# Latent mixer of a fused two-block kernel: value products for two query tiles at once, and a pad on the right-hand side of SBUF

## The chip, the cores and the metric

The kernel runs on one core of a Trainium2 chip. The metric is the device time of one execution in microseconds (us). Beside it stands one profiled execution, from which all rows below come. The engines are named as in the profile: PE is TensorE, PEld its weight loads, DVE VectorE, ACT ScalarE, POOL GpSimd, SP SyncE.

## The reference, cut to what matters

The program computes two blocks one after the other: first two layers of attention, mLSTM and MLP on 512 tokens, then a second block whose first mixer is multi-head latent attention and whose second is a gated linear scan. The change lies in the latent mixer. It has 16 heads, 512 tokens (`hx`) and 256 context tokens (`hc`). Queries and keys have 64 + 32 elements, values 64. The context attends to itself alone, the tokens attend to context and tokens together (768 keys):

```python
def attention_blocks(q, k, v):
...
    def one_block(qi):
        s = jnp.einsum('bqhrd,bkhd->bhrqk', qi, k, preferred_element_type=F32) * scale
        p = jax.nn.softmax(s, axis=-1).astype(v.dtype)
        return jnp.einsum('bhrqk,bkhe->bqhre', p, v)
...
def mla_mixer(hc, hx, row, col, w_in, q_norm_g, w_uq, kv_norm_g, w_ukv, w_out):
...
    oc = attention_blocks(qc, kc, vc)
    ox = attention_blocks(qx, jnp.concatenate([kc, kx], axis=1), jnp.concatenate([vc, vx], axis=1))

    def out(o, gate):
        b, n, _ = gate.shape
...
```

The result is multiplied by the gate's silu and taken through the output weight.

## The kernel before, in words

All work runs on one core, and the products carry nearly all of it. Most are made of three by `mm3` (lines 280, 281 and 282: high part by high part, high by low, low by high), each operand split into a high and a low part by `split` (lines 251 to 255). The profile shows these three lines with the names of the destination and of the operands: `S<-kT,qT` are scores, `T<-cqT,spl` the queries, `T<-ckT,spl` the keys, `A<-spl,hi` the mixer's output products.

`mla` is the latent mixer. Its attention goes through 8 pairs of heads `hp`. Each pair has five steps: a context step (`c=1`, both context query tiles at once, 256 keys) and four query tiles of 128 tokens with 768 keys (`t0` 0 to 3; called tiles 0 to 3 here, and the two heads of a pair a and b).

- `softmax` makes the scores of one head into a PSUM buffer `S` (two of them), the negated row maximum on DVE (line 1211), the exponential with its row sum on ACT (line 1216, which the profile shows as ACTIVATE and ACTIVATION_READ_ACCUMULATOR), the reciprocal and the multiply on DVE (lines 1218 and 1221), once for head a and once for head b.
- `weigh` runs one step behind. It transposes the normalised weights 128 by 128 on PE (line 1236, six for a head and a tile), copies them on ACT to `pt` (line 1237, 512 and 256 columns), and then multiplies them with the values into a quarter of the PSUM buffer `O` (line 1244: six blocks of keys by two heads, 128 columns each, head a into partitions 0 to 63 and head b into 64 to 127).
- `prepare(hp+1)` makes the queries and keys of the next pair in small pieces that are taken up between these steps. A pair with an even number has its pieces in the context step and tile 0, a pair with an odd number in tile 1 too, and pair 7 has none.

The order of each engine's instructions is set when the program is built, by the tile framework's list scheduler from the code's order and the buffers' reuse; it isn't written out by hand. Buffers on the left and right side of SBUF are stacked one beside the other: `res` is the first pool on the right (`side="right"`), so everything that is allocated there behind it stands at an offset that `res` fixes. Among these are the mixer's `cqT`, `ckT` (in place of which `hi` comes later), `V`, `sg` and the raw weights. They stand at 224 bytes past a multiple of 256.

Of the kernel before, what the change touches and what calls it, by code (L numbers as in the profile page):

```python
# [10 lines left out]
F32 = mybir.dt.float32  # L11
# [3 lines left out]
AF = mybir.ActivationFunctionType  # L15
# [181 lines left out]
class Prog:  # L197
    def __init__(self, tc, A, ctx):
        self.tc, self.nc, self.A, self.ctx = tc, tc.nc, A, ctx
        self.const = self.pool("const", 1)  # L200
        self.res = self.pool("res", 1, side="right")
        self.raw = self.pool("raw", 2, side="right")
        self.spl = self.pool("spl", 4)
        self.sm = self.pool("sm", 4)
        self.mhalf = self.const.tile([128, 4], F32, name="mhalf")
        self.nc.gpsimd.memset(self.mhalf, -0.5)
        self.zero = self.const.tile([128, 1], F32, name="zero")
        self.nc.gpsimd.memset(self.zero, 0.0)
# [841 lines left out]
def mla(P, xs, mod, H, before, keep):  # L1050

    nc, A = P.nc, P.A
# [13 lines left out]
    with ExitStack() as s1:  # L1066
# [33 lines left out]
        for j in range(8):  # L1100
            w = W().rearrange("p s (k n) -> p s k n", k=8)
            for c, o, n in PARTS:
                ps = P.bankA()[:, 0:n]
                for k in range(8):
                    P.mm3(ps, w[:, 0, k], w[:, 1, k], *H.all(k, c), k == 0, k == 7)
                v = sg[j][:, o:o + n]
# [3 lines left out]
    before.close()  # L1110
    with st as s2:
        P.psum(s2, S=(2, 2), T=(3, 1), O=(1, 1))
        kp, pp, one, qp = (P.pool(*x, s2) for x in (("m2k", 3), ("m2p", 3), ("m2o", 1), ("m2q", 4)))
        kTs = [one.tile([96, 2, 768], F32R, name=f"kT{i}") for i in (2, 3, 0, 1)]
        kTs = kTs[2:] + kTs[:2]
        tab = one.tile([128, 512], F32, name="tab")
# [1 line left out]
        V = [vp.tile([128, 1024], F32, name="V") for _ in range(6)]  # L1118
# [7 lines left out]
        for c, o, n in PARTS:  # L1126
            pt = P.bankT()
# [97 lines left out]
        def weigh(hp, c, t0, ps):  # L1225
            two, m, c0 = (2, 256, 512) if c else (1, 768, 0)
            if t0 == 0:
                weigh.o = P.bankO()
            pts = []
            for p in ps:  # L1230
                pt = kp.tile([128, 768], F32, name="pt")
                for o in range(0, two * m, 512):
                    w = min(512, two * m - o)
                    pst = P.bankT()
                    for k in range(0, w, 128):
                        nc.tensor.transpose(pst[:, k:k + 128], p[:, o + k:o + k + 128], P.ident)  # L1236
                    nc.scalar.activation(pt[:, o:o + w], pst[:, 0:w], AF.Copy)  # L1237
                pts.append(pt)
                yield
            for t in range(two):  # L1240
                for k in range(m // 128):
                    for i in range(2):
                        h = 2 * hp + i
                        nc.tensor.matmul(weigh.o[64 * i:64 * i + 64, (t0 + t) * 128:(t0 + t + 1) * 128],  # L1244
                                         V[4 * c + k][:, h * 64:(h + 1) * 64],
                                         pts[i][:, t * m + k * 128:t * m + (k + 1) * 128],
                                         start=(k == 0), stop=(k == m // 128 - 1))
            n = 256 if c else 512
            if (t0 + two) * 128 == n:
                v = sg[hp][:, c0:c0 + n]  # L1250
                nc.vector.tensor_tensor(v, v, weigh.o[:, 0:n], op=OP.mult)
# [3 lines left out]
        for hp, c, t in steps:  # L1255
            if c:
                ready = prepare(hp + 1) if hp < 7 else iter(())
            sm = softmax(hp, c, t)
            w = weigh(*before) if before else iter(())
            next(w, None)  # L1260
            for _ in range(2):
                ps = next(sm)
                next(ready, None)
                next(w, None)
            before = (hp, c, t, ps)
        alternate(weigh(*before))


# [325 lines left out]
def program(tc, A, out):  # L1594
    with ExitStack() as ctx:
        P = Prog(tc, A, ctx)
        xs = [P.res.tile([128, 1024], F32, name=f"x{t}") for t in range(4)]
        before, keep = ExitStack(), ExitStack()
        H, mod = first_block(P, xs, P.pool("hx", 1, before))
        finish = mla(P, xs, mod.m[0], H, before, keep)  # L1600
        gla(P, xs, finish, keep, mod.m[1], out)
# [18 lines left out]
```

## Time and profile before

| | |
|---|---|
| time, median of 3 runs | 2332.73 us (2332.15 to 2332.93) |
| the profiled execution | 2335.07 us |
| its span | 2333.3 us, 1.8 us less than the execution |
| PE busy in the span | 2284.1 us (98%) |
| weight loads (PEld) | 1875.9 us (80%) |
| DVE | 1478.0 us (63%) |
| ACT | 1063.0 us (46%) |
| attention of the latent mixer | from about 1686 to 1934 us |

An engine is busy while it runs an instruction; a PE row's time is that of its instruction from start to end, and neighbours overlap, so that the distance from one start to the next is what a product costs the stream. "x24" joins 24 records of one kind in a row. Each float32 product of a value group leaves two records. The granted clock of TensorE is the share of full speed.

### The profile page before, as it was taken

To read this page: it belongs to the slowest core of one execution; us is meant where nothing else is said; L and a number is where in the kernel's file an instruction comes from. 1 tells how busy PE (TensorE), PEld (TensorE's weight loads), DVE (VectorE), ACT (ScalarE), POOL (GpSimd) and SP (SyncE) were. 2 spreads that over 40 slices of the span, in tenths; PEclk is the share of its full clock that TensorE was granted. 3 is DMA by queue.
4 is the path that set the end of the run, shared out by engine and by line. 5 is a ranking of instruction groups with operands and counts; after the bars stand their busy time and mean duration, and the time that the engine had idled before them with its cause. 6 is when DMAs were issued, how large, how long until landed. Compare 5 with 4: busy or idle time off the path is not lost.

```text
span 2333.3 us, 30784 instructions
## 1 busy us (share of the span) xinstructions
PE 2284.1 (98%) x12108; PEld 1875.9 (80%) x12108; DVE 1478.0 (63%) x2556; ACT 1063.0 (46%) x1958; POOL 71.4 (3%) x120
## 2 busy tenths in 40 slices
PE   8999999999999999999999999999999999999998
PEld 6777878888888777788888888888888888788886
DVE  4477796555555547779645556564478776756586
ACT  3366423444443235642344445452477772563332
POOL 0000000000000000000000000010000000000000
PEclk9999999999999999999999999999999999999999
DMA  4221464555642322146454554212110121121112
GB/s 162 81 73 55 145 212 142 167 130 151 174 100 91 92 81 75 52 155 216 135 172 120 160 164 116 92 54 72 49 31 21 24 74 37 54 81 37 55 46 72
DMA packets 61312, 234.38 MB, mean 100 GB/s; under 512 B 8544, under 2 KB 9840, under 8 KB 54768
## 3 DMA queue, kind: packets, MB, share of 16 engines
q1 hardware_dynamic: 50512, 179.99, 23.3%
q0 software_dynamic: 3456, 25.17, 6.0%
q10 hardware_dynamic: 7200, 27.27, 3.7%
q8 instruction: 95, 1.56, 0.3%
q14 instruction: 49, 0.40, 0.1%
HBM read 227.15 MB, written 2.10 MB: 98 GB/s over the span
## 4 chain that ended last, share of the span: by engine, by line
PE 81%; DVE 10%; ACT 3%; DMA 3%; issue 2%; POOL 1%; SPq 0%; POOLq 0%; ACTq 0%; DVEq 0%
PE A L282 18%; PE A L281 18%; PE A L280 18%; PE S L280 4%; PE S L282 4%; PE S L281 4%; PE O L1244 2%; DVE spl L252 2%; PE T L1236 2%; PE O L522 1%; DMA ada<-in_ada 1%; PE S L496 1%; DVE junk L933 1%; PE T L516 1%; ACT spl L251 1%
## 5 line engine op out<-in xcount | busy, mean ns | idle before, releaser
L280 PE MATMUL A<-big,spl 128*128 128x512 f32 (+1 forms) x1280 | 482.2, 377 | 1.9 <-DVE x L768 1.2
L282 PE MATMUL A<-big,spl 128*128 128x512 f32 (+1 forms) x1280 | 481.0, 376 | 0.2 <-DVE spl L252 0.2
L281 PE MATMUL A<-big,spl 128*128 128x512 f32 (+1 forms) x1280 | 480.1, 375 | 0.0
L252 DVE TENSOR_TENSOR spl<-raw,spl 128x1024 fp32r<-128x1024 f32 (+2 forms) x265 | 317.2, 1200 | 184.0 <-ACT spl L251 182.2
L251 ACT ACTIVATE spl<-raw 128x1024 fp32r<-128x1024 f32 (+2 forms) x265 | 275.2, 1040 | 292.2 <-PE A L282 190.6
L282 PEld LDWEIGHTS A<-big,spl 128*128 128x128 f32 x1280 | 241.2, 188 | 44.6 <-issue 2.6
L280 PEld LDWEIGHTS A<-big,spl 128*128 128x128 f32 x1280 | 241.3, 189 | 43.9 <-DVE x L768 1.6
L281 PEld LDWEIGHTS A<-big,spl 128*128 128x128 f32 x1280 | 241.3, 189 | 42.5 <-issue 1.4
L252 DVE TENSOR_TENSOR spl<-quarter,spl 128x1024 fp32r<-128x1024 f32 x84 | 102.2, 1223 | 144.9 <-ACT spl L251 144.9
L280 PE MATMUL A<-spl,big 128*128 128x512 f32 (+2 forms) x480 | 182.7, 384 | 3.7 <-DVE tg L668 2.1
L281 PE MATMUL A<-spl,big 128*128 128x512 f32 (+2 forms) x480 | 182.3, 381 | 1.4 <-DVE spl L252 0.8
L282 PE MATMUL A<-spl,big 128*128 128x512 f32 (+2 forms) x480 | 181.7, 380 | 0.2 <-DVE ms L289 0.2
L251 ACT ACTIVATE spl<-quarter 128x1024 fp32r<-128x1024 f32 x84 | 88.2, 1057 | 97.4 <-PE S L282 41.1
L280 PEld LDWEIGHTS A<-spl,big 128*128 128x128 f32 x480 | 90.2, 189 | 23.2 <-DVE tg L668 3.0
L281 PEld LDWEIGHTS A<-spl,big 128*128 128x128 f32 x480 | 90.7, 189 | 18.9 <-DVE spl L252 3.4
L282 PEld LDWEIGHTS A<-spl,big 128*128 128x128 f32 x480 | 90.6, 189 | 16.7 <-issue 1.1
L280 PE MATMUL S<-spl,part 128*128 128x512 f32 x264 | 102.8, 389 | 0.0
L281 PE MATMUL S<-spl,part 128*128 128x512 f32 x264 | 102.8, 389 | 0.0
L282 PE MATMUL S<-spl,part 128*128 128x512 f32 x264 | 102.8, 389 | 0.0
L1211 DVE TENSOR_REDUCE mx<-S 128x1 f32<-128x768 f32 (+1 forms) x80 | 71.8, 900 | 26.5 <-PE S L282 25.7
L291 POOL TENSOR_TENSOR rstd<-ms,mhalf 128x1 f32<-128x1 f32 (+2 forms) x68 | 44.2, 650 | 1247.5 <-DVE ms L289 1203.2
L1237 ACT ACTIVATE pt<-T 128x512 f32<-128x512 f32 (+1 forms) x144 | 66.4, 501 | 32.4 <-PE T L1236 31.2
(442 smaller groups left out, 4349.2 us busy)
## 6 DMA issues: line engine op xcount, KB each, us to landing
raw<-in_wl SPq DMA_DIRECT2D x196, 512.0 KB, 3.7
ada<-in_ada ACTq DMA_DIRECT2D x48, 512.0 KB, 4.0
quarter<-in_wq SPq DMA_DIRECT2D x24, 1024.0 KB, 6.2
quarter<-in_wq POOLq DMA_DIRECT2D x24, 1024.0 KB, 8.7
raw<-in_gla SPq DMA_DIRECT2D x33, 512.0 KB, 3.4
raw<-in_mla SPq DMA_DIRECT2D x20, 512.0 KB, 3.5
raw<-in_mla SPq DMA_DIRECT2D x8, 384.0 KB, 3.0
qT<-rot SPq DMA_DIRECT2D x32, 96.0 KB, 2.8
```

The source lines that it names most:

```text
L251: nc.scalar.activation(hi, src, AF.Copy)
L252: nc.vector.tensor_tensor(lo, src, f32(hi), op=OP.subtract)
L280: mm(ps, lh, rh, start=start, stop=False, **more)
L281: mm(ps, lh, rl, start=False, stop=False, **more)
L282: mm(ps, ll, rh, start=False, stop=stop, **more)
L291: nc.gpsimd.tensor_tensor(r, ms, self.mhalf[:, 0:w], op=OP.pow)
L496: nc.tensor.matmul(banks[hh][:, 0:w], qT[hs, i, q], kT[hs, j, 0:w], start=(i + j == 0), stop=(i == 1))
L516: nc.tensor.transpose(psp[:, k * 128:(k + 1) * 128], p[:, k * 128:(k + 1) * 128], P.ident)
L1211: nc.vector.tensor_reduce(mx[:, 0:two], pss[:, 0:two * m].rearrange("p (t n) -> p t n", t=two), AX.X, OP.max, negate=True)
L1236: nc.tensor.transpose(pst[:, k:k + 128], p[:, o + k:o + k + 128], P.ident)
L1237: nc.scalar.activation(pt[:, o:o + w], pst[:, 0:w], AF.Copy)
L1244: nc.tensor.matmul(weigh.o[64 * i:64 * i + 64, (t0 + t) * 128:(t0 + t + 1) * 128], V[4 * c + k][:, h * 64:(h + 1) * 64], pts[i][:, t * m + ...
```

## The change

Two things are changed. First, `weigh` collects two query tiles: `pt` becomes a tile of 6 blocks of keys by 2 query tiles by 128 columns, the copies write every second block of it, and the products with the values are issued after every second query tile, with 256 moving columns (both tiles at once). In the context step the two context tiles go together in the same way. The pool of `pt` has four buffers in place of three. Second, a tile of 56 float32 columns (224 bytes) is allocated first in `res`.

```diff
@@ Prog.__init__
         self.res = self.pool("res", 1, side="right")
+
+        self.res.tile([128, 56], F32, name="pad")
         self.raw = self.pool("raw", 2, side="right")
@@ mla
-        kp, pp, one, qp = (P.pool(*x, s2) for x in (("m2k", 3), ("m2p", 3), ("m2o", 1), ("m2q", 4)))
+        kp, pp, one, qp = (P.pool(*x, s2) for x in (("m2k", 4), ("m2p", 3), ("m2o", 1), ("m2q", 4)))
@@ weigh
-            pts = []
-            for p in ps:
-                pt = kp.tile([128, 768], F32, name="pt")
+
+            if t0 % 2 == 0:
+                weigh.pts = [kp.tile([128, 6, 2, 128], F32, name="pt") for _ in range(2)]
+            pts = weigh.pts
+            for p, pt in zip(ps, pts):
                 for o in range(0, two * m, 512):
                     w = min(512, two * m - o)
                     pst = P.bankT()
                     for k in range(0, w, 128):
                         nc.tensor.transpose(pst[:, k:k + 128], p[:, o + k:o + k + 128], P.ident)
-                    nc.scalar.activation(pt[:, o:o + w], pst[:, 0:w], AF.Copy)
-                pts.append(pt)
+                    if c:
+                        d, v = pt[:, 0:2], pst.rearrange("p (t k n) -> p k t n", t=2, k=2)
+                    else:
+                        d, v = pt[:, o // 128:(o + w) // 128, t0 % 2], pst[:, 0:w].rearrange("p (k n) -> p k n", n=128)
+                    nc.scalar.activation(d, v, AF.Copy)
                 yield
-            for t in range(two):
+            if c or t0 % 2:
+                q = slice(0, 256) if c else slice((t0 - 1) * 128, (t0 + 1) * 128)
                 for k in range(m // 128):
                     for i in range(2):
                         h = 2 * hp + i
-                        nc.tensor.matmul(weigh.o[64 * i:64 * i + 64, (t0 + t) * 128:(t0 + t + 1) * 128],
-                                         V[4 * c + k][:, h * 64:(h + 1) * 64],
-                                         pts[i][:, t * m + k * 128:t * m + (k + 1) * 128],
+                        nc.tensor.matmul(weigh.o[64 * i:64 * i + 64, q], V[4 * c + k][:, h * 64:(h + 1) * 64],
+                                         pts[i][:, k].rearrange("p t n -> p (t n)"),
                                          start=(k == 0), stop=(k == m // 128 - 1))
```

The scheduler puts the work in another order around it. In the listings below an instruction has its line, destination and sources; the change adds two lines ahead of `mm3` and more within `weigh`, so that line 1244 becomes 1252, 1236 becomes 1240, and 280 to 282 become 282 to 284. The keys of head a and head b of pair 0 are `kT_12892` and `kT_12893` before, and `kT_12893` and `kT_12894` in the changed kernel.

On PE, head pair 0, from the scores of tile 1, head b, to those of tile 2, head b, before:

```order
L282 MATMUL S<-kT_12893,qT 128x256
L1244 MATMUL O<-pt,V 64x128 x12
L280 MATMUL S<-kT_12892,qT 128x512
L281 MATMUL S<-kT_12892,qT 128x512
L1236 MATMUL T<-ident,p 128x128 x6
L282 MATMUL S<-kT_12892,qT 128x512
L280 MATMUL S<-kT_12892,qT 128x256
L281 MATMUL S<-kT_12892,qT 128x256
L282 MATMUL S<-kT_12892,qT 128x256
L1236 MATMUL T<-ident,p 128x128 x6
```

and in the changed kernel, up to the value products of tiles 0 and 1:

```order
L284 MATMUL S<-kT_12894,qT 128x256
L282 MATMUL S<-kT_12893,qT 128x512
...
L284 MATMUL S<-kT_12893,qT 128x256
L1240 MATMUL T<-ident,p 128x128 x6
L282 MATMUL S<-kT_12894,qT 128x512
...
L283 MATMUL S<-kT_12894,qT 128x256
L1240 MATMUL T<-ident,p 128x128 x6
L284 MATMUL S<-kT_12894,qT 128x256
L1252 MATMUL O<-pt,V 64x256 x12
L1240 MATMUL T<-ident,p 128x128 x6
```

The 12 products with the values stood between the scores of tile 1 and those of tile 2; now the scores of tile 2 follow those of tile 1 at once, and the products of both tiles come after the transposes of tile 1.

On DVE, head pair 0, the maxima (1211, afterwards 1213), reciprocals and multiplies of tile 1 and the beginning of tile 2, before:

```order
L1211 TENSOR_REDUCE mx<-S 128x1 x2
L1218 RECIPROCAL sl<-sl 128x1
L1221 TENSOR_SCALAR p<-p,sl 128x768
L1218 RECIPROCAL sl<-sl 128x1
L1221 TENSOR_SCALAR p<-p,sl 128x768
L1211 TENSOR_REDUCE mx<-S 128x1 x2
```

and in the changed kernel:

```order
L1213 TENSOR_REDUCE mx<-S 128x1
L1220 RECIPROCAL sl<-sl 128x1
L1223 TENSOR_SCALAR p<-p,sl 128x768
L1213 TENSOR_REDUCE mx<-S 128x1
L1220 RECIPROCAL sl<-sl 128x1
L1223 TENSOR_SCALAR p<-p,sl 128x768
```

Between the multiply of head a and that of head b of tile 1 now stands the maximum of tile 2, head a.

On PE, the end of head pair 0, from the scores of tile 3, head b, to the context scores of the next pair (keys `kT_12890`, in the changed kernel `kT_12891`), before:

```order
L282 MATMUL S<-kT_12893,qT 128x256
L1244 MATMUL O<-pt,V 64x128 x12
L280 MATMUL S<-kT_12890,qT 128x256
L281 MATMUL S<-kT_12890,qT 128x256
L282 MATMUL S<-kT_12890,qT 128x256
L1236 MATMUL T<-ident,p 128x128 x6
```

and in the changed kernel:

```order
L284 MATMUL S<-kT_12894,qT 128x256
L282 MATMUL S<-kT_12891,qT 128x256
L283 MATMUL S<-kT_12891,qT 128x256
L284 MATMUL S<-kT_12891,qT 128x256
L282 MATMUL S<-kT_12891,qT 128x256
L283 MATMUL S<-kT_12891,qT 128x256
L284 MATMUL S<-kT_12891,qT 128x256
L1240 MATMUL T<-ident,p 128x128 x6
```

Here too the 12 products between the two groups of scores are gone; those of tiles 2 and 3 come in the next pair's context step.

## Rows read from the trace of the kernel before

**Rows 1.** The page, first part: busy us, share of the span, instructions.
```profile
PE 2284.1 (98%) x12108; PEld 1875.9 (80%) x12108; DVE 1478.0 (63%) x2556; ACT 1063.0 (46%) x1958; POOL 71.4 (3%) x120
```

**Rows 2.** Windows, attention stage: length, busy by engine, PE clock, DMA share, GB/s.
```profile
core 0: us, PE busy (x) PEld busy (x) DVE busy (x) ACT busy (x) POOL busy (x), PEclk, DMA share, GB/s
1686.00:1934.00 248.00, 245.75 (x2068) 206.71 (x2066) 190.46 (x362) 179.92 (x408) 0.00 (x0) 1.00 0.14 36
```

**Rows 3.** Timeline, PE, pairs 0 and 1: start, us, instruction [idle before].
```profile
1697.69 0.28 PE L282 MATMUL S<-kT,qT 96*128 96x256 f32 x1
1697.90 1.53 PE L1244 MATMUL O<-pt,V 128*64 128x128 f32 x24
1699.36 0.50 PE L280 MATMUL S<-kT,qT 96*128 96x512 f32 x1
1699.70 0.40 PE L281 MATMUL S<-kT,qT 96*128 96x512 f32 x1
1699.93 0.82 PE L1236 MATMUL T<-ident,p 128*128 128x128 f32 x6
...
1701.06 0.28 PE L282 MATMUL S<-kT,qT 96*128 96x256 f32 x1
1701.18 0.82 PE L1236 MATMUL T<-ident,p 128*128 128x128 f32 x6
1701.75 0.48 PE L280 MATMUL S<-kT,qT 96*128 96x512 f32 x1
...
1712.26 0.36 PE L280 MATMUL S<-kT,qT 96*128 96x256 f32 x1
...
1722.87 1.09 PE L1244 MATMUL O<-pt,V 128*64 128x128 f32 x16
```

**Rows 4.** Timeline, PE, gated scan: float32 products of 256 columns.
```profile
2194.49 1.03 PE L1534 MATMUL O<-S,qk 128*128 128x256 f32 x4
2195.36 0.60 PE L1532 MATMUL O<-vx,acc 128*128 128x256 f32 x2
```

**Rows 5.** Lines of ACT by form: busy, mean ns of one, idle before, releaser.
```profile
L1237 ACT ACTIVATE pt<-T 128x512 f32<-128x512 f32 x80 | 47.8, 597 | 32.3 <-PE T L1236 31.2
L251 ACT ACTIVATE big<-T 128x512 fp32r<-128x512 f32 x32 | 18.1, 593 | 16.0 <-PE T L757 15.8
```

**Rows 6.** Line 281: ns of one, minimum, median, maximum, by operands.
```profile
L281 PE MATMUL S<-spl,part x264: 388/389/390, 487.5 to 1475.6; 128*128 128x512 f32 x132
...
L281 PE MATMUL A<-spl,hi x96: 392/396/482, 1930.7 to 2006.7; 128*128 128x512 f32 x96
```

**Rows 7.** Timeline, PE, attention stage: first and last of eight neighbours.
```profile
1794.38 0.40 PE L281 MATMUL T<-cqT,spl 128*128 128x512 f32 x1
...
1796.01 0.40 PE L282 MATMUL T<-cqT,spl 128*128 128x512 f32 x1
```

**Rows 8.** Timeline, DVE, head pair 0, tile 1.
```profile
1698.01 0.96 DVE L1211 TENSOR_REDUCE mx<-S 128x1 f32<-128x768 f32 x1 [0.29 <-PE S L282]
...
1699.07 0.62 DVE L1221 TENSOR_SCALAR p<-p,sl 128x768 f32<-128x768 f32 x1
```

**Rows 9.** Timeline, ACT, head pair 0, tiles 1 and 2.
```profile
1697.76 0.90 ACT L1216 ACTIVATE p<-S,mx 128x768 f32<-128x768 f32 x1 [0.34 <-DVE mx L1211]
1698.56 0.19 ACT L1216 ACTIVATION_READ_ACCUMULATOR p<-S,mx 128x1 f32 x1
...
1705.70 0.87 ACT L1237 ACTIVATE pt<-T 128x512 f32<-128x512 f32 x2 [0.64 <-PE T L1236]
```

**Rows 10.** Timeline, PE, head pair 1.
```profile
1732.78 1.14 PE L1236 MATMUL T<-ident,p 128*128 128x128 f32 x6
...
1736.61 1.85 PE L1244 MATMUL O<-pt,V 128*64 128x128 f32 x24
```

**Rows 11.** Timeline, PE, head pair 7, context step.
```profile
1906.06 0.87 PE L1236 MATMUL T<-ident,p 128*128 128x128 f32 x6 [0.23 <-DVE p L1221]
1907.61 0.50 PE L280 MATMUL S<-kT,qT 96*128 96x512 f32 x1 [0.67 <-ACT p L1216]
```

**Rows 12.** Timeline, ACT, head pair 7: what ended ahead of the last row.
```profile
1907.36 0.20 ACT L1216 ACTIVATION_READ_ACCUMULATOR p<-S,mx 128x1 f32 x1
```

## The prediction

> **What bounds the kernel now.** I read the page's first part, then the engines' busy time in the attention stage of the latent mixer, then that stage row by row. TensorE (PE) is busy 2284.1 of the span's 2333.3 us [rows 1], and in the stage from 1686 to 1934 us it is busy 245.75 of 248.00 us at a granted clock of 1.00, while DVE has 190.46 and ACT 179.92 [rows 2]. So the bound is PE's stream of matmuls, and its order is fixed when the program is built. But DVE and ACT are loaded to three quarters there, and each query tile runs a chain through them (row maximum on DVE, exponential on ACT, reciprocal and multiply on DVE, transposes on PE, copies on ACT). That chain is hidden only as long as PE has other work queued between its links. The question is therefore twofold: what PE has less to do, and whether the cover still lies where the chain needs it.
>
> **The change part by part.** *Fewer, wider value products.* A group of 12 products prints as 24 records (each of these float32 products leaves two), because the two heads' halves run side by side. The group takes from 1697.90 to the next start at 1699.36, 1.46 us [rows 3]. Its 12 slots: the busy 1.53 us of 24 records less the 1.09 of 16 is .44 for four slots, .11 each (.109 with the unrounded rows) [rows 3], so 1.31 for 12 and about .15 for getting into and out of the group. Its entry costs .21 where two neighbours of 256 columns stand .12 apart, and its exit .34 where two 512-column neighbours stand .23 apart; with the slot's own slack I take .33 for a group in all [rows 3]. With 256 columns a float32 record takes (2195.36 - 2194.49)/4 = .217 us, from the only such products in the trace [rows 4]. The mixer has 448 slots now (896 records), 224 afterwards: 448 x .109 = 48.8 against 224 x .216 = 48.4, a gain of only .4 us. The columns streamed stay the same. What does fall is the number of groups in the order: 56 to 37, so 19 x .33 = 6.3. **PE's work falls by 6.7 us.**
>
> What one slot costs is read here from rows: 24 records in 1.46 us are .061 us a record, and no more than the entry and exit above is lost beside the columns [rows 3]. The Trainium skill (TensorE: Matmul & The Clock Gate, section Back-to-back issue gap) says that in a stream of weight load and matmul pairs a 128-column matmul comes every 81 ns or so, because the load takes its share. By that, halving the records would be worth an estimated 448 x (81 - 53) ns = 12.5 us in place of .4; the trace's 61 ns do not agree with it.
>
> *Copies that write two tiles interleaved.* The new copies write 128x4x128 with a stride. ACT's copy of transposed blocks into `big` has such a strided destination already and takes 593 ns at 128x512, the plain copy of `pt` 597 [rows 5]. Cost zero, bounds -.01 to +.01 us on 144 copies, so under 1.5 either way, all of it off PE's path.
>
> *The pad.* 56 columns of float32 move what stands on the right from 224 to 0 past a multiple of 256 bytes. The operands that moved so far stand at 224 and their 512-column products cost a little more: `A<-spl,hi` has a median of 396 ns, `S<-spl,part`, whose moving operand stands aligned already, 389 [rows 6]; in a row without a break the `T<-cqT,spl` products start (1796.01 - 1794.38)/7 = .233 us apart [rows 7]. 172 products on each of the three lines of `mm3` (288 of `hi` and `lo`, the rest of `cqT` and `ckT`) become aligned: 516 x 6 ns = **-3.1 us**. Products of 256 columns I cost at nothing, for their spacing is .12 in both cases. Bounds: 0 (the difference comes from something else) and 516 x 7 = -3.6.
>
> *What is moved, and the waits this opens.* Value products of a first tile now wait for the second one. In the order PE's place between the scores of one tile and those of the next, which the 12 products filled for 1.46 us, is empty after every first tile. I walked the new order by hand through head pair 0, from 1697.69, up to where both orders are the same, with the durations of the rows: scores of one head 3 x .23 + 3 x .118 = 1.04, six transposes .57 [rows 3], maximum .96, multiply .62 [rows 8], exponential and accumulator read to 1698.56 + .19 = 1698.75, two copies .87 [rows 9], some .05 for each hop between engines.
> - Scores of tile 2, head a, need the PSUM buffer of tile 1, head a, which is free when the accumulator has been read: 1698.75 + .05 [rows 9]. PE is there at 1697.81. **Wait .99.** Before, the value products lay exactly here.
> - They end at 1699.84, so the maximum of tile 2 runs on DVE 1700.04 to 1701.00, and in DVE's new order it stands ahead of the multiply of tile 1, head b, which ends 1701.82. PE, finished with its scores at 1701.42, waits for it: **.45**.
> - The value products of the pair (12 x .216) follow the second head's copies by less than before: **.3**.
> - At the end of the pair, the scores of the next head pair's context tile follow directly; their buffer waits for the exponential of tile 3, head a, which stands behind ACT's copies of tile 2 (.87): **.85**. Then the multiply of tile 3, head a, on DVE: **.43**. Then **.1** before the last transposes.
>
> In sum 3.1 us for an even head pair. By the walk its last transposes of tile 3 end at 1713.23 against 1712.26 where before the next scores start [rows 3], +.97, and 24 records of 256 columns are then still to come against 24 of 128: 2.59 - 1.31 = +1.28. So **+2.25 for each of the four even pairs**, with the gain from groups inside it. The odd pairs 1, 3 and 5 have products of `prepare` in tile 1, which cover the first wait, so 2.2 us of waits; their own stalls of before go away (.32 in transposes of 1.14 instead of .82, .32 in value products of 1.85 instead of 1.53) [rows 10]; three groups fewer give .99, the slots .1: **+.45 each**. Pair 7 has no filler and the same waits, but it already stood .23 and .67 behind the multiply and the exponential at its start [rows 11], and it has three groups fewer: I take **+.5**, bounds 0 and 1. Both rows [rows 11] show that such waits do come when cover is short, and with ACT's row that the buffer comes free when the accumulator read ends (1907.36 + .20, PE starts at 1907.61) [rows 12].
>
> Sum: 4 x 2.25 + 3 x .45 + .5 = +10.85, pad -3.1, **+7.75 us**. The profiled execution took 2335.07 us (span 2333.3 and 1.8 around it), so it would be 2342.8; the median of the runs is 2332.73, 2.34 below it, so **2340.5 us**.
>
> **The rivals.** *A, the other side: cover suffices.* If the tensor queue's slack (DVE done earlier, or hops shorter than I count) hides the waits after first tiles, what stays is -6.7 - 3.1 = -9.8: 2322.9 us. It decides at the first wait: the exponential of tile 1 would have to end before 1697.81, while it does not start before 1697.76 [rows 9]. That row speaks against it, as does 1907.61; for it speaks only that a walk of five steps through three engines may miss a rearrangement later. *B, half the waits.* The waits of the walk are 4 x 3.1 + 3 x 2.2 + 3.3 = 22.3 us. Each one delays PE and by that gives DVE and ACT time, so a later wait can be paid by an earlier one, above all the .43, .45 and .3. With half of them the time is 2340.5 - 11 = 2329.5, no change to measure. *C, the pad does nothing.* The 6 ns could belong to the weights' side or to the tile's row length. Then 2343.6. The Trainium skill (SBUF — State Buffer, section Door 1: The DMA port swizzle) speaks of lines of 16 bytes as the unit that an access pays for; 224 is a multiple of 16, so by that page alone the pad would do nothing. The medians of 396 and 389 [rows 6] are against it. *D, the waits cascade*: ACT's copies, an engine at 180 of 248 us, come later in every pair and delay the next exponentials: twice the two end waits in each pair, some 7 x .6 = +4, 2344.7.
>
> **How the numbers follow.** Chances: forecast .42, A .15, B .25, C .12, D .06. A measurement of this kernel can tell some 0.2% (4.7 us) from no change, which is 2328.1 to 2337.4. Faster: A and a part of B below its middle, .20. Same: the rest of B and the lower end of the forecast, .25. Slower: .55. The range leaves out A and the far ends of C and D: low 2326, high 2346. The forecast's own range is 2337 to 2344.
>
> **What would show it.** Right: in the changed profile, in the mixer's attention stage, PE's scores have waits for the exponential (ACT `p`) and its transposes waits for the multiply (DVE `p`), three to five of .3 to 1 us in each even pair, and PE's busy share falls there while the stage is 10 us longer; the value products come as 448 records of about .216 us with the same sum; products with `cqT` and `hi` show 389 instead of 396. Wrong: no wait ahead of the scores of tile 2 (then A), waits of half that sum (B), medians unmoved (C), or time lost in the first block or after the mixer, where the order and the operands but for the pad are as before.

## The result, and the profile after

The changed kernel takes 2348.3 us (median of four runs, 2346.18 to 2350.33) against 2332.83 for the kernel before: 1.0066 times the time, 95% interval 1.0054 to 1.0078. It is slower, by twice the amount forecast (15.5 us instead of 7.75) and above the range. The profiled execution took 2349.28 us with a span of 2347.5, 14.2 more than the span before.

The page's line on the engines and the attention stage, for [rows 1, 2]. The windows' columns are length, busy time by engine, granted clock, DMA share and GB/s:

```profile
PE 2287.3 (97%) x11660; PEld 1860.7 (79%) x11660; DVE 1476.2 (63%) x2556; ACT 1059.7 (45%) x1958; POOL 71.4 (3%) x120
```

```profile
1686.00:1934.00 248.00, 235.83 (x1527) 181.51 (x1526) 181.76 (x348) 168.50 (x392) 0.00 (x0) 0.99 0.14 36
```

PE has 448 records fewer and yet is busy 3.2 us longer. In the same window of 248 us it is now busy 235.83 instead of 245.75 us, and the mean granted clock has fallen a little. The waits of PE in the attention stage (releaser, total us, how many, the longest), of the changed kernel, whose stage is longer (1686 to 1950 us):

```profile
PE S L282 <- ACT p L1218: 9.2, 15, 1.6
PE T L1240 <- DVE p L1223: 3.2, 7, 1.9
PE S L282 <- issue: 0.7, 1, 0.7
PE O L1252 <- ACT pt L1245: 0.3, 1, 0.3
```

Before, the same list (1686 to 1934 us) had 1.1 us in three waits and 1.0 in three. These are the two kinds that the forecast named: scores waiting for the exponential, transposes waiting for the multiply. Head pair 0 on PE (start, us, instruction, in brackets the idle time before it), for [rows 3]:

```profile
1698.82 0.28 PE L284 MATMUL S<-kT,qT 96*128 96x256 f32 x1
1699.69 0.50 PE L282 MATMUL S<-kT,qT 96*128 96x512 f32 x1 [0.59 <-ACT p L1218]
...
1702.47 0.28 PE L283 MATMUL S<-kT,qT 96*128 96x256 f32 x1
1702.79 0.87 PE L1240 MATMUL T<-ident,p 128*128 128x128 f32 x6
1703.42 0.36 PE L284 MATMUL S<-kT,qT 96*128 96x256 f32 x1
1703.71 3.22 PE L1252 MATMUL O<-pt,V 128*64 128x256 f32 x24
1706.87 0.87 PE L1240 MATMUL T<-ident,p 128*128 128x128 f32 x6
...
1710.22 0.28 PE L284 MATMUL S<-kT,qT 96*128 96x256 f32 x1
1711.18 0.36 PE L282 MATMUL S<-kT,qT 96*128 96x256 f32 x1 [0.69 <-issue]
...
1714.33 0.37 PE L282 MATMUL S<-kT,qT 96*128 96x256 f32 x1
```

The last scores of tile 1 start at 1698.82, .12 later PE could go on, and the scores of tile 2 start at 1699.69: .75 us where the walk had .99. On ACT the exponential that they wait for, for [rows 9]:

```profile
1698.64 0.91 ACT L1218 ACTIVATE p<-S,mx 128x768 f32<-128x768 f32 x1
1699.43 0.21 ACT L1218 ACTIVATION_READ_ACCUMULATOR p<-S,mx 128x1 f32 x1
```

The accumulator read ends at 1699.64 and PE starts at 1699.69, as [rows 11, 12] had it. The scores with the next pair's keys come .84 us after PE was free (1710.34), as the walk's .85; the profile names no releaser there ("issue"). Measured from 1698.82, which answers to 1697.69 before, the scores behind the pair's last transposes stand at 1714.33 instead of 1712.26, that is 2.07 - 1.13 = .94 later; the walk said .97.

### Pair by pair

The table follows the first score product of tile 1 through the traces. Each figure is by how much the kernel falls further behind the kernel before from one pair's tile 1 to the next pair's (for pair 7 to 1936 us in the trace of before). The third and fourth columns are experiments that have the same order on PE and come below.

| head pair | walk | changed kernel | pairing without pad | hi split on POOL |
|---|---|---|---|---|
| 0 | 2.25 | 2.11 | 2.16 | 2.11 |
| 1 | .45 | .74 | .78 | .72 |
| 2 | 2.25 | 2.14 | 2.19 | 2.16 |
| 3 | .45 | 1.69 | 1.74 | 1.68 |
| 4 | 2.25 | 2.27 | 2.33 | 2.27 |
| 5 | .45 | .48 | .51 | .46 |
| 6 | 2.25 | 3.92 | 3.70 | 2.36 |
| 7 | .5 | 3.35 | 1.75 | 3.28 |
| sum | 10.85 | 16.7 | 15.2 | 15.0 |

Pairs 0, 2, 4, 1 and 5 are as walked, within .3. The 5.85 us that the walk lacks are in pairs 3, 6 and 7. In pairs 6 and 7 stand the two longest waits of PE, ahead of two falls of the granted clock (windows of the changed kernel, same columns):

```profile
1901.46 0.28 PE L284 MATMUL S<-kT,qT 96*128 96x256 f32 x1
1903.37 0.50 PE L282 MATMUL S<-kT,qT 96*128 96x512 f32 x1 [1.62 <-ACT p L1218]
...
1942.64 0.28 PE L284 MATMUL S<-kT,qT 96*128 96x256 f32 x1
1944.78 1.51 PE L1240 MATMUL T<-ident,p 128*128 128x128 f32 x6 [1.87 <-DVE p L1223]
```

```profile
1902.00:1904.00 2.00, 0.64 (x2) 0.57 (x3) 1.36 (x3) 2.00 (x5) 0.00 (x0) 0.94 0.00 0
1904.00:1906.00 2.00, 2.00 (x10) 1.83 (x9) 0.95 (x3) 1.12 (x4) 0.00 (x0) 0.50 0.00 0
1906.00:1908.00 2.00, 2.00 (x12) 1.91 (x12) 0.96 (x1) 1.76 (x4) 0.00 (x0) 0.71 0.03 8
1944.00:1946.00 2.00, 1.22 (x7) 1.25 (x7) 1.61 (x7) 1.03 (x3) 0.00 (x0) 0.68 0.00 0
1946.00:1948.00 2.00, 2.00 (x9) 1.70 (x8) 0.09 (x2) 0.78 (x2) 0.00 (x0) 0.50 0.03 8
```

PE is idle for 1.62 us, busy .64 of 2.00, and from about 1904 to 1907 its clock is granted at .50, which is 1.2 GHz; six transposes that take .82 us elsewhere take 1.51 here. The kernel before has no such stretch in this stage (1.00 in [rows 2]). The executions of the changed kernel whose mean clock was .997 have spans of 2344.4 and 2345.5 us, those at .996 have 2347.5 and 2348.5.

The stage's 16.7 us are more than the span's 14.2: another 1.5 us were lost by 1668 us, ahead of the changed code, and 3.9 came back after the mixer's attention (both below).

### The profile page after: what moved, and what is told of

It is laid out like the page before. It is cut to its first block, busy times and chain, and to the rows that moved or that the text cites. A ratio compares the mean times of both kernels' runs of the same rounds, so it can differ in the third digit from the quotient of the medians.

```text
span 2347.5 us, 29861 instructions
## 1 busy us (share of the span) xinstructions
PE 2287.3 (97%) x11660; PEld 1860.7 (79%) x11660; DVE 1476.2 (63%) x2556; ACT 1059.7 (45%) x1958; POOL 71.4 (3%) x120
## 3 DMA queue, kind: packets, MB, share of 16 engines
q8 instruction: 92, 1.51, 0.3%
## 4 chain that ended last, share of the span: by engine, by line
PE 81%; DVE 10%; ACT 4%; DMA 2%; issue 2%; POOL 1%; SPq 0%; ACTq 0%; POOLq 0%; DVEq 0%
PE A L284 17%; PE A L283 17%; PE A L282 17%; PE S L282 4%; PE S L284 4%; PE S L283 4%; PE O L1252 2%; PE T L1240 2%; DVE spl L254 2%; PE O L524 1%; DMA ada<-in_ada 1%; PE S L498 1%; DVE junk L935 1%; PE T L518 1%; ACT spl L253 1%
## 5 line engine op out<-in xcount | busy, mean ns | idle before, releaser
L1218 ACT ACTIVATE p<-S,mx 128x768 f32<-128x768 f32 (+1 forms) x96 | 72.7, 760 | 25.9 <-DVE mx L1213 24.1
```

The lines of the kernel that those rows point to most:

```text
L1218: nc.scalar.activation(p[:, t * m:(t + 1) * m], pss[:, t * m:(t + 1) * m], AF.Exp, bias=mx[:, t:t + 1], accum_out=sl[:, t:t + 1])
```

## The experiments

All compare with the kernel before on the same chip; times are medians.

### Pad alone, pairing alone

```diff
+        self.res.tile([128, 56], F32, name="pad")
```

> The kernel before with the pad alone. Theory (operand starts matter, waits come from the pairing): 516 products of 512 columns get 6 ns shorter, -3.1 us, about 2329.7; products with hi and cqT at 389 instead of 396 ns, and no waits of TensorE in the attention stage beyond those of before. Rival (the pad shifts something that costs, as the first 60 us of the changed kernel, 1.2 us later than before, might suggest): 2333 or more.

2330.64 against 2333.34 us, ratio .9992 (.9983 to 1.0001): -2.7 by the medians and -1.9 by the ratio, near the forecast in size, but its interval just holds no change. In the trace the mechanism is plain (line 281 or 282: minimum, median, maximum ns; kernel with the pad), for [rows 6]:

```profile
L282 PE MATMUL S<-spl,part x264: 389/389/389, 485.4 to 1473.4; 128*128 128x512 f32 x132
...
L282 PE MATMUL A<-spl,hi x96: 387/389/481, 1928.1 to 2002.6; 128*128 128x512 f32 x96
```

The products with `hi` went from 396 to 389, as those of the changed kernel did. Those with `cqT` only did so in part: of the 99 products `T<-cqT,spl` with 512 columns the median is 396 before, 395 with the pad alone, where the expectation had 389, and 389 in the changed kernel. Compared product by product, the kernel with the pad gains 1.4 us on the kernel before while the products of `hi` and `lo` run (1936 to 2010 us), .4 us from 1600 us to the attention, and nothing within the attention.

> The changed kernel without the pad: pairing alone. Theory: the pairing loses its 18 or so us with or without the pad, and 3.1 us more for the operand starts: about 2351.5. Rival (pad is what hurts): 2348 or less.

The changed kernel without its pad line took 2351.0 against 2333.34 us, ratio 1.0076 (1.0062 to 1.009): +17.7, and 2.7 more than with the pad. So the pad comes out near its forecast, with the reservations above, and all of the loss is the pairing's. The clock falls here too, once, in pair 6: 13 us behind that pair's long wait, which left it at 1.00, and right behind a wait of .76 us:

```profile
1905.98 0.51 PE L280 MATMUL S<-kT,qT 96*128 96x512 f32 x1 [1.61 <-ACT p L1216]
...
1919.13 0.47 PE L280 MATMUL S<-kT,qT 96*128 96x256 f32 x1 [0.76 <-ACT p L1216]
```

```profile
1918.00:1920.00 2.00, 1.24 (x8) 1.04 (x7) 1.68 (x6) 1.85 (x6) 0.00 (x0) 0.82 0.74 250
1920.00:1922.00 2.00, 2.00 (x12) 2.00 (x11) 1.91 (x5) 1.87 (x5) 0.00 (x0) 0.50 0.03 12
1922.00:1924.00 2.00, 2.00 (x10) 1.32 (x9) 1.05 (x2) 1.06 (x3) 0.00 (x0) 0.82 0.30 51
```

Its pair 7, with the same wait of 1.87 us at its end and no fall, loses 1.75 us instead of 3.35 (table). A fall costs 1.6 us there.

### The same tile and copies, products after each tile

```diff
-            if c or t0 % 2:
-                q = slice(0, 256) if c else slice((t0 - 1) * 128, (t0 + 1) * 128)
+            for t in range(two):
                 for k in range(m // 128):
                     for i in range(2):
                         h = 2 * hp + i
-                        nc.tensor.matmul(weigh.o[64 * i:64 * i + 64, q], V[4 * c + k][:, h * 64:(h + 1) * 64],
-                                         pts[i][:, k].rearrange("p t n -> p (t n)"),
+                        nc.tensor.matmul(weigh.o[64 * i:64 * i + 64, (t0 + t) * 128:(t0 + t + 1) * 128],
+                                         V[4 * c + k][:, h * 64:(h + 1) * 64], pts[i][:, k, t if c else t0 % 2],
```

> The changed kernel (pad, pt tile for two query tiles, copies that write with a stride, four buffers) but with value products of 128 columns right after each tile, as before. Theory (the cover is what is missing): the waits of the changed kernel are gone, and the time is that of the pad alone, 2329 to 2331. Rival (strided copies or the larger pt tile cost): 2335 or more, with longer copies on ScalarE.

2330.65 us, the time of the pad alone (2330.64). The copies with a stride cost nothing (597 ns at 512 columns, 597 in [rows 5]), nor do the larger tile and the fourth buffer. What costs is that the products come two tiles at a time.

### Products of 256 columns, spread over the steps

```diff
...
+            while left:
+                a = left.pop(0)
+                if a[1]:
+                    a[4] = P.bankO()
+                products(*a)
+            if c:
+                left.append([hp, c, t0, pts, None, range(2), True])
+            elif t0 % 2:
+                if t0 == 1:
+                    weigh.o = P.bankO()
+                products(hp, c, t0, pts, weigh.o, range(3), False)
+                left.append([hp, c, t0, pts, weigh.o, range(3, 6), t0 == 3])
...
```

> The changed kernel with 256-column products, but those of a pair of tiles in two halves, three key blocks after the second tile and three one step later, and the context's one step later too, so that some products stand in nearly every step. Theory (place, not width): the waits mostly vanish, 2324 to 2331 (pad -3.1, fewer groups up to -5, what waits remain on top). Rival (256 columns cost by themselves, as slots that drift apart or a longer stream): 2338 or more, with TensorE busy longer and no waits.

2337.27 against 2333.34 us, ratio 1.0016 (1.0007 to 1.0025). Between the two theories: 11 us of the loss are gone, and so are the waits (the four groups of the list above have become these two),

```profile
PE S L282 <- ACT p L1218: 1.0, 2, 0.7
PE T L1253 <- DVE p L1223: 0.8, 2, 0.4
```

but 6.6 us more than the pad alone remain, and the waits (1.8 us, against 1.6 with the pad alone) don't show them. That is where torn groups come in.

### Torn groups

Value products of head a and head b run side by side. The scheduler puts a first product of head a where it is free early, and the group is then torn after an odd number. In the changed kernel:

```profile
1715.21 0.65 PE L1252 MATMUL O<-pt,V 128*64 128x256 f32 x2
1715.79 0.50 PE L282 MATMUL T<-ckT,spl 128*128 128x512 f32 x1
...
1717.37 2.80 PE L1252 MATMUL O<-pt,V 128*64 128x256 f32 x22
1720.11 0.66 PE L1240 MATMUL T<-ident,p 128*128 128x128 f32 x4
```

Two records (one product) take .58 to the next start and 22 take 2.74, together 3.32 for 12 slots of .216, or .36 in each piece beside its slots. A whole group costs .15 beside its slots, in both kernels (1.46 - 12 x .109 in [rows 3]). The difference is one slot: a lone product has no partner, and it is .10 with 128 columns and .21 with 256. A group can also be whole in the listing and still have lone products: the first group of pair 0 above begins and ends with one and takes 3.16 us, .57 beside its slots. Counted over the traces, 34 of 56 groups held a lone product before (32 with an odd number, two whole ones) and 30 of 37 afterwards (26 and four). Beside their slots all groups together cost 14.1 us before and 13.1 after, of which 1.0 and .1 are waits.

```diff
                 for k in range(m // 128):
-                    for i in range(2):
+                    for i in (1, 0):
                         h = 2 * hp + i
```

With head b first no product can be placed before both heads' copies are there. This was put to the changed kernel, to the spread-out one and to the pad alone.

> The changed kernel with head b's product first: 24 whole groups instead of 37, of which most are torn and cost .36 beside their slots. Theory (the forecast's 6.3 us for fewer groups didn't come because torn groups of 256 columns lose a slot of .216): 13.1 - 24 x .153 = 9.4 us less, 2339, waits for the exponential as before. Rival (the time is in the waits alone, groups don't matter): 2346 to 2350.

2338.82 against 2333.72 us, ratio 1.0023 (1.0015 to 1.0032): 9.5 us less than the changed kernel, against 9.4 expected. The first group of pair 0 has no lone product now and takes 2.74 instead of 3.16 us:

```profile
1702.46 2.81 PE L1252 MATMUL O<-pt,V 128*64 128x256 f32 x24
1705.20 0.88 PE L1240 MATMUL T<-ident,p 128*128 128x128 f32 x6
```

The waits for the exponential are what they were (9.1 us), and those for copies have grown from .3 to 2.2. That the figure was met so closely is partly chance, because the clock has a part in it: in this profile it falls once in the attention, 1.1 us behind pair 6's wait of 1.62 us, where the changed kernel has two falls,

```profile
1898.00:1900.00 2.00, 2.00 (x12) 1.95 (x11) 0.86 (x3) 1.69 (x5) 0.00 (x0) 0.56 0.00 0
1900.00:1902.00 2.00, 2.00 (x10) 1.82 (x9) 0.88 (x1) 1.75 (x4) 0.00 (x0) 0.58 0.04 8
```

and two falls of the changed kernel behind the mixer (at 2044 and 2126 us) do not come. From tile 1 of pair 0 to 1936 us of the trace of before, this kernel falls 8.3 us behind instead of 16.7.

> The staggered kernel (256-column products in halves over the steps) with head b's product first: 44 groups, all even, instead of 60. Theory: 17.8 - 44 x .153 = 11.1 us less than the 2337.3 of the staggered kernel, 2326, a little above the pad with head b first, for the same number of groups. Rival (its loss is in the chain through DVE and ScalarE): 2335 or more.

2330.42 against 2333.72 us, ratio .9984 (.9975 to .9993): 6.9 less than with torn groups, where 11.1 were expected; all groups together cost 7.2 us beside their slots instead of 17.8, while PE's waits grow from 1.8 to 2.9 us. The other 3 us or so are not accounted for. This is the time of the pad alone, whose groups are torn; the kernel that it has to be held against is the next one.

> The pad alone, and in each value product group head b's product ahead of head a's, so that no product can be placed before both heads' copies are there. In the kernel before, groups that are torn after an odd number of products cost .25 us beside their slots, whole ones .15, and there are 56 of them; here 44, all even. Theory (torn groups cost a slot each): 14.1 - 44 x .153 = 7.4 us less, 2323 unless waits take their place. Rival (the early products fill gaps for free): as with the pad alone, 2330, or slower by new waits for copies.

2327.5 against 2333.72 us, ratio .9973 (.9963 to .9983): faster than both kernels, by 3.1 us more than the pad. Groups cost 8.1 us beside their slots instead of 14.1, and PE's waits in the stage grow from 1.6 to 2.7 us. Less than half of the 7.4 us came; what took the rest is open. With whole groups on both sides, and 44 of them each, the spread-out kernel of 256 columns (2330.42) takes 2.9 us more than this one: the wide products gain nothing and lose a little. The changed kernel with whole groups (2338.82) takes 11.3 us more, so that of the pairing's loss of 17.7 us against the pad alone some 6 hang on the torn groups.

### Splits on ScalarE

```diff
-            P.split(hi[hp], lo[hp], sg[hp])
+            nc.gpsimd.tensor_copy(hi[hp], sg[hp])
+            nc.vector.tensor_tensor(lo[hp], sg[hp], f32(hi[hp]), op=OP.subtract)
```

> The changed kernel with the high parts of the mixer's output operand (hi from sg) made on GpSimd instead of ScalarE. Three of these splits (.84 us each) stand on ScalarE ahead of an exponential in head pair 6, where TensorE waits 1.62 us and its granted clock then falls to 0.50 for 3.4 us. Theory (splits on ScalarE, then the clock, make pair 6's loss): that wait falls under .9, the clock stays at 1.00 around 1904 us, and 2 to 4 us come back: 2344 to 2346. Rival (the wait is from the lost cover alone, as in pair 0, and the splits don't matter): wait and time as in the changed kernel, 2347 to 2349.

The explanation falls, although the time came out near its figure: 2346.52 against 2333.72 us, ratio 1.0054 (1.0041 to 1.0067). The wait of pair 6 is there unchanged,

```profile
1901.55 0.50 PE L282 MATMUL S<-kT,qT 96*128 96x512 f32 x1 [1.64 <-ACT p L1218]
```

but the clock stays at 1.00 behind it and falls only at the end of pair 7:

```profile
1902.00:1904.00 2.00, 1.91 (x12) 1.48 (x10) 2.00 (x5) 1.47 (x4) 0.00 (x0) 1.00 0.18 27
1942.00:1944.00 2.00, 2.00 (x11) 1.66 (x10) 0.84 (x5) 0.87 (x2) 0.00 (x0) 0.58 0.03 8
1944.00:1946.00 2.00, 2.00 (x8) 0.63 (x6) 0.00 (x0) 0.87 (x2) 0.00 (x0) 0.56 0.00 0
```

So pair 6 without a fall loses 2.36 us, nearly the walk's 2.25, and with one 3.70 and 3.92: the fall costs 1.3 to 1.6 us. Pair 6 has this wait, 1.61 to 1.64 us, in four profiles: the clock falls within 1.1 us behind it in the changed kernel and with head b first, and does not in the pairing alone and here. Pair 7's wait of 1.87 us is in all four too, with a fall in the changed kernel and here. What decides it is not shown.

### A shorter chain

```diff
-                mx = P.sm.tile([128, 2], F32, name="mx")
-                nc.vector.tensor_reduce(mx[:, 0:two], pss[:, 0:two * m].rearrange("p (t n) -> p t n", t=two),
-                                        AX.X, OP.max, negate=True)
...
-                                         bias=mx[:, t:t + 1], accum_out=sl[:, t:t + 1])
+                                         scale=2.0 ** -10, accum_out=sl[:, t:t + 1])
```

> The pad alone, with the row maximum left out of the latent mixer's softmax (no DVE maximum; the exponential takes the scores divided by 1024, so that nothing overflows): a part of the computation is left out, only to shorten the chain between scores and transposes by about 1.2 us a head and tile. All theories: nearly the time of the pad alone, 2327 to 2331, since few waits are there to take away (1.6 us in the stage).

> The changed kernel with the same part left out (no row maximum, scores divided by 1024). Theory (the pairing loses by a chain through DVE and ScalarE that has lost its cover): the waits of the changed kernel shrink to under 4 us in all, the clock stays at 1.00, and the time comes near that of the pad with the same part left out, within 3 us either way. Rival (the wide products, torn groups or other costs on TensorE itself make the loss): 8 us or more above it, with TensorE busy.

Both kernels leave out the row maximum and divide the scores by 1024, so they don't compute the mixer's softmax; they only show what the shorter chain is worth. The pad with the shorter chain takes 2319.69 us against 2333.25 (.9943, .9928 to .9957), the changed kernel with the shorter chain 2321.59 (.995, .9935 to .9964). The pairing's 17.7 us shrink to 1.9. The waits that are left with the pairing:

```profile
PE T L1237 <- DVE p L1220: 1.4, 5, 0.3
PE S L282 <- ACT p L1215: 0.5, 2, 0.3
PE O L1249 <- ACT pt L1242: 0.2, 1, 0.2
```

and the clock is 1.00 throughout the stage. So most of the pairing's loss is the chain through DVE and ACT that has lost its cover; the wide products themselves cost at most these 1.9 us. The shorter chain also changed the groups, to 7.8 us beside their slots with the pairing and 7.6 without, so these two runs don't part waits from torn groups; the two kernels with head b first do, 11.3 us apart. The first of the two expectations missed: the pad's kernel was to change little and became 11 us faster. Its order changed with the chain, and its groups cost 7.6 us beside their slots instead of 14.1; that would be 6.5 of the 11 if all of it came through, which no run shows.

### Another pad

```diff
+        self.res.tile([128, 40], F32, name="pad")
```

> The pad with 40 columns instead of 56: operands on the right at 64 past a multiple of 256 bytes instead of 0. Theory A (multiples of 64 bytes are enough): products with hi have a median of 389 ns, time as with the pad of 56 columns, 2330. Theory B (256 is needed): 396 ns and 2333.

2333.66 against 2333.25 us (1.0001, .9992 to 1.0011):

```profile
L282 PE MATMUL A<-spl,hi x96: 391/394/481, 1930.3 to 2006.3; 128*128 128x512 f32 x96
```

The median is 394 ns, neither 389 nor 396, but the mean of these 96 products is 396, as before, against 390 with the pad of 56 columns. A start at 64 past a multiple of 256 bytes gives back nothing that can be measured, in the products or in the time (theory B). The Trainium skill (SBUF — State Buffer, section Door 1: The DMA port swizzle) makes lines of 16 bytes the unit that an access pays for. All three starts (224, 64 and 0 past a multiple of 256) are multiples of 16, and their medians are 396, 394 and 389 ns; the measurement decides. For the products the rival that the pad does nothing is out; for the time of the pad alone the interval just holds it.

## Why the prediction was wrong

The sign and the mechanism were right: PE loses its cover after every first tile and waits for the exponential and the multiply. The size was not. The sum "4 x 2.25 + 3 x .45 + .5 = +10.85" stands against 16.7 us in the trace, and three of its steps failed.

- **The clock was left out of the sum.** The step "I walked the new order by hand" priced a wait at its own length. Two waits, 1.62 and 1.87 us, were followed by a granted clock of .50, at 1.3 to 1.6 us each. They are 3 of the missing 5.85 us in the stage. The clock of [rows 2] is that of a stage whose longest wait was .67 us. The sum had no term for a slower clock. Yet the trace of the kernel before held two such falls behind the mixer, at 2028 and 2110 us, where the forecast didn't look. The second (PE, and two windows behind it):

```profile
2108.81 1.56 PE L1488 MATMUL L<-qk 128*128 128x128 f32 x8 [1.91 <-DVE acc L1471]
```

```profile
2110.00:2112.00 2.00, 2.00 (x12) 2.00 (x11) 1.60 (x3) 0.00 (x0) 0.00 (x0) 0.58 0.00 0
2112.00:2114.00 2.00, 2.00 (x7) 1.58 (x6) 1.95 (x5) 0.77 (x2) 0.00 (x0) 0.57 0.00 0
```

- **Pairs 3 and 7 were not walked.** Pair 0 was, and it came out within .14, as did pairs 2 and 4 that repeat it. Part of that is luck: the six waits of pair 0 come to 2.2 us from start to start (.75, .20, .08, .84, .30 and .02) where the walk had 3.1, and the first value group takes 3.16 us where the walk had 12 x .216 = 2.59. Pair 7 ("I take +.5, bounds 0 and 1") loses 1.75 even without a fall, with a wait of 1.87 at its end where the kernel before has 24 records of tile 2 ahead of the last transposes and waits .41. Of the odd pairs the changed kernel takes 35.51, 35.50 and 35.51 us for pairs 1, 3 and 5, but the kernel before 34.76, 33.81 and 35.03: "their own stalls of before go away" took those of pair 1 [rows 10] for all three, and pair 3 had hardly any to give. It loses 1.7 instead of .45, for this and the next reason.
- **Fewer groups were worth nothing.** "What does fall is the number of groups [...] 19 x .33 = 6.3" took one price for every group. It is .15 for a whole one and .36 for a torn one, and the slot that a torn group loses doubles with the columns: 14.1 us before, 13.1 after. In the odd pairs and in pair 7 the sum counted it ("three groups fewer give .99"). In pair 3 the groups of the kernel before cost 1.7 us beside their slots and those of the changed kernel 1.8, so none of the .99 came. Rival A, 2322.9, rested on the same gain. Making the groups whole took 9.5 us off the changed kernel.

What held: the slot (.216 for 256 columns, 65.6 us of product records before and 63.8 after, so halving the records was worth next to nothing) and the copies with a stride at nothing. By the Trainium skill's 81 ns for a matmul of 128 columns in a stream of loads and matmuls (TensorE: Matmul & The Clock Gate, section Back-to-back issue gap) halving them would have been worth an estimated 12.5 us; the trace does not agree with it. The pad at -3.1 came out at -2.7, but only 1.8 us of it can be seen where the operands that it moves are used, and the interval holds no change. Also, in the products with `hi` ([rows 6]) the pad moves the weights; their moving operand, the split output weight, stands on the left. The cases B and D had no part in it: the waits were not halved, and they did not cascade in pairs 0, 2 and 4.

A part of the difference is not the change's. By 1655 us, ahead of the mixer's attention, the changed kernel stands 1.6 us behind the kernel before, the pad alone 2.3 us ahead and the pairing alone 3.6 behind, with the same code there. Of the 3.6 us 2.7 are longer waits of PE for split weights (4.3 instead of 1.6 us), of the 2.3 us 1.6 are its first long wait (8.5 instead of 10.1 us). After the mixer 1.5 us come back with the products of `hi` and `lo`, in the kernels with the pad of 56 columns only, and another 1.5 at 2258 us, also in the pairing without the pad: there PE waits 1.34 us for ACT's `ka` before and not afterwards, for a reason that isn't shown. The medians, 15.5 us and for the pairing alone 17.7, differ from what the attention loses in the two profiles, 16.7 and 15.2, by no more than such shifts and one fall of the clock.

## What to carry to other kernels

Work that is bundled to save instructions also leaves the places where it hid a chain through other engines; walk one whole period of the new order with the durations of the trace, and then each period that differs from it, the last above all. Where two streams run side by side on PE, issue first the one whose operand comes last, so that the scheduler can't tear the group: that was worth 3.1 us here beside the pad alone, and with the pad 6.2 us (ratio .9973), while the bundling gained nothing in any form.

## What the runs showed of the hardware

- A lone float32 product of 64 output columns costs a whole slot more than one of a pair that runs on both halves: .10 us with 128 moving columns, .21 with 256.
- Four kernels have waits of PE of 1.6 and 1.9 us in pairs 6 and 7. Four of these eight waits were followed within 1.1 us by a fall of the granted clock to .50, four were not, and one more fall stood right behind a wait of .76 us. A fall cost 1.3 to 1.6 us.
- Products of 512 columns whose operand starts 224, 64 and 0 bytes past a multiple of 256 have medians of 396, 394 and 389 ns and means of 396, 396 and 390 (line 281 of before, `A<-spl,hi`).
